# A hybrid sequence block: the modulation's matrix as TensorE's stationary float32 operand

## The chip, the cores and the metric

The kernel runs on one core of one Trainium2 chip. The metric is the device time of one execution in microseconds (us), the median of the runs shown.

## The reference

The block takes 2048 latent tokens `x` and 256 context tokens `ctx`, each of 1024 channels. A condition vector gives shift, scale and gate by one matrix product, once for `c` and once for `c_ctx`; the normed tokens are scaled and shifted by them, projected, mixed by four branches (a gated linear recurrence, a short convolution, a Fourier transform, a state space model) and projected back; the gate scales what is added to `x`.

```python
def adaln(cvec, ada_w, ada_b):
    m = jax.nn.silu(cvec) @ ada_w + ada_b
    m = m.reshape(-1, 1, 3 * D_MODEL)
    return jnp.split(m, 3, axis=-1)
...
shift, scale, gate = adaln(c, ada_w[l], ada_b[l])
h = rmsnorm(x, norm_w[l]) * (1.0 + scale) + shift
out, _, _ = mix(h, lp, rows, rg_st, ssd_st)
x = x + gate * out
```

`ada_w` is 1024 x 3072 in float32: 8 MB for shift and scale, 4 MB for the gate.

## The kernel before, in words

All large products run on TensorE (PE) as three products of float32r operands, `mm3` (L141 to L144): each float32 operand is split into a high part (a copy by ScalarE, `copy_hi`, L139) and a rest (a subtraction by VectorE or GpSimd), and high by high, high by rest and rest by high are summed in PSUM. Every instruction of the program is put in order on its engine when the kernel is compiled, by a scheduler that estimates times (`schedule_with_timeline_sim=True`); each engine then runs its own queue strictly in that order. Loads and stores are all issued from SyncE's queue (`ld`, L134).

**First stage.** The shift and scale columns come in eight blocks `k` of 1 MB (`ada_load`, two loads of 512 KB each), each with 128 shift and 128 scale columns for channels 128k to 128k+127. Two blocks share one of the 16 KB slots `H2` to `H5`. `ada_block` (L273) splits a block into slot `H6` or `H7`: in two halves of four row tiles, ScalarE copies the high part, VectorE subtracts three row tiles and GpSimd one (L281). The conditions stand still in PE: 4 columns (the high parts and the rests of `silu(c)` and `silu(c_ctx)`, `sil4`) for the matrix' high part (L283, 8 products of 256 moving columns) and 2 columns for its rest (L285, 8 more). The sum, 4 rows of 256, is copied to SBUF (L287) and transposed in two pieces (L289) into the bank `apt`, where three small VectorE operations (L292 to L294) turn it into `mod[k]`: shift, and norm weight times (1 + scale).

`to_h` (L298) then transposes channels 128k to 128k+127 of 512 normed tokens (four PE transposes, L301), applies `mod[k]` (`hr`, L305 or L307) and splits the result (`h_hi`, L139; `h_lo`, L309). In the loop over `k`, `ada_block(k)`, `to_h(k)` and nine products of three weight blocks with these 512 tokens (`mm3` into three accumulating banks) follow each other in the program. Behind the loop come the context's tokens (`xc`, loaded into slot `H2`), the next 512 tokens (`x1`, loaded into slot `H4`, which the blocks 4 and 5 held), and further products. Their loads stand behind the last block's in SyncE's queue.

**The gate's stage.** The gate's 1024 columns are worked out much later, beside the state space model's chain of states (L750 on): for each half of the columns and each of eight row tiles, 256 KB of the matrix are loaded (`gst`, two buffers), split by ScalarE and GpSimd (L214) and multiplied by `mm3` with a single stationary column (48 products of 512 moving columns). The sum lies in a bank of tag `bb`, of which there are two; before it, the same tag serves the products of L715 and L730. The row is added to the bias (L759) and stored.

Of the kernel before, what the change touches and what calls it, by code (L numbers as in the profile page):

```python
# [8 lines left out]
F32 = mybir.dt.float32  # L9
# [6 lines left out]
T = 2048  # L16
# [17 lines left out]
def constants():  # L34
# [5 lines left out]
    # channel transform: [cos 0..64 | sin 0..63], with the ortho norm and the gate's half  # L40
# [6 lines left out]
    # token transform: rows in blocks (window of 256, parity)  # L47
# [10 lines left out]
    # [par*4+w][cos/sin][128][f] -> split f into two tiles  # L58
# [11 lines left out]
def layout(x, c, ctx, c_ctx, ada_w, ada_b, norm_w, w_in, w_out, rg_conv_w, rg_conv_b, rg_gate_a_w, rg_gate_a_b,  # L70
# [7 lines left out]
    # [block of columns k][row within 128][rows / 128][shift | scale]  # L78
    a["ada"] = ca(ada_w[0][:, :2048].reshape(8, 128, 2, 8, 128).transpose(3, 1, 0, 2, 4).reshape(8, 128, 8, 256))
    a["adag"] = ca(ada_w[0][:, 2048:].reshape(8, 128, 1024))  # L80
    a["adabg"] = ca(ada_b[0][None, 2048:])
# [40 lines left out]
def build(tc, A, out):  # L122
# [23 lines left out]
    def softplus(pl, x, n, dst, scale_in=1.0, tag=None, bufs=None):  # L146
        """dst = log(1 + exp(scale_in * x)) for a [128, n] tile, exact also where it is small."""
# [27 lines left out]
    def mbank(four):  # L175
        """a bank for a projection; with four, of those of the transposes too"""
        nbank[0] += 1
        return bank("tr" if four and nbank[0] % 2 else "mm")
# [7 lines left out]
    # ---------------------------------------------------------------- constants  # L186
# [20 lines left out]
    # ---------------------------------------------------------------- weight blocks  # L207
# [3 lines left out]
    def split(hi, lo, raw, eng):  # L211
        """raw (float32) as a high part and a rest, both of 12 bits"""
        copy_hi(hi, raw)
        eng.tensor_tensor(lo, raw, f32(hi), SUB)  # L214
# [20 lines left out]
    # ---------------------------------------------------------------- adaLN shift and scale  # L235
# [10 lines left out]
    def norm_rows(xt):  # L246
        """scales the rows of xt [128, 1024] by 1/rms"""
        junk = q1.tile([128, 1024], BF16, name="junk")
        ss, rs = one("ss"), one("rs")
        act.activation(junk, xt, AF.Square, accum_out=ss)  # L250
        dve.tensor_scalar(rs, ss, 1.0 / D, EPS, MUL, ADD)
        pool.tensor_tensor(rs, rs, mhalf, ALU.pow)
        dve.tensor_scalar(xt, xt, rs, None, MUL)
        return xt

    # high and low part of the four columns side by side: one pass over the matrix' high part serves both
    sil4 = cst.tile([128, 8, 4], F32R, name="sil4")
    copy_hi(sil4[:, :, 0:2], sil)
    dve.tensor_tensor(sil4[:, :, 2:4], sil, f32(sil4[:, :, 0:2]), SUB)
# [4 lines left out]
    # [k][:, who] = shift, norm_w * (1 + scale)  # L264
# [7 lines left out]

    def ada_block(ar, k):  # L273
        hl = H16(f"ada{k}", 6 + k % 2, F32R, (2, 8, 256))
        pa = bank("ba")
        for i in range(2):
            s4 = slice(4 * i, 4 * i + 4)
            copy_hi(hl[:, 0, s4], ar[:, s4])
            for j, eng in ((0, dve), (1, pool)):
                r = slice(4 * i + 3 * j, 4 * i + 3 + j)  # L280
                eng.tensor_tensor(hl[:, 1, r], ar[:, r], f32(hl[:, 0, r]), SUB)  # L281
            for j in range(4 * i, 4 * i + 4):
                pe.matmul(pa[0:4, :256], sil4[:, j], hl[:, 0, j], start=(j == 0), stop=False)  # L283
            for j in range(4 * i, 4 * i + 4):
                pe.matmul(pa[0:2, :256], sil4[:, j, 0:2], hl[:, 1, j], start=False, stop=(j == 7))  # L285
        arow = q1.tile([4, 256], F32, name="arow", tag="arow", bufs=2)
        dve.tensor_copy(arow, pa[0:4, :256])  # L287
        for j in range(2):
            pe.transpose(apt[:, 8 * k + 4 * j:8 * k + 4 * j + 4], arow[:, 128 * j:128 * (j + 1)], ident[0:4, 0:4])  # L289
        av = apt[:, 8 * k:8 * k + 8].rearrange("p (j w) -> p w j", w=4)  # L290
        m = mod[k]
        dve.tensor_tensor(m, av[:, 0:2], adab[:, k, None, :].to_broadcast([128, 2, 2]), ADD)  # L292
        dve.tensor_tensor(m, m, av[:, 2:4], ADD)
        dve.tensor_scalar(m[:, :, 1], m[:, :, 1], cols[:, C_NW + k:C_NW + k + 1], None, MUL)  # L294

    # ---------------------------------------------------------------- normed, modulated, transposed tokens
# [30 lines left out]
    def conv_silu(pl, b, projs, n, emit, nb=3):  # L327
        """causal-ish convolution of 4 taps and silu over consecutive tiles of n tokens, each then given to emit"""
# [48 lines left out]
    # ---------------------------------------------------------------- first columns: RG-LRU input, context  # L377
# [30 lines left out]
    # the first tile of tokens and three blocks of weights run along with the columns of the modulation's matrix  # L408
# [9 lines left out]
    x1 = H16("x1", 4, F32, (4, 1024))  # L418
# [25 lines left out]
    # dt of the context, by columns  # L444
# [45 lines left out]
    # ---------------------------------------------------------------- RG-LRU  # L490
# [13 lines left out]
    def rg_front(us, n, e2):  # L504
        """Units of n tokens, at most one of either direction, each (blk, d, gate weights, source, conv, keep, init):
        the decays, the gated inputs and, in e2, the squares of these inputs' factors. A unit with conv starts from
        raw columns; their convolution goes to keep."""
        u = r2("r_u", 2)
        al = slice(us[0][1], us[-1][1] + 1)
        for blk, d, g, src, conv, keep, init in us:  # L510
            if conv:
                # two columns before and one after, zero beyond the ends
# [37 lines left out]
    def rg_back(us, n, e2, a, v, spans):  # L550
        """half the states of the units; the second to pass over a span of tokens adds the first one's"""
# [45 lines left out]
    for first in units:  # L597
        # two at a time, for the sake of one square root
# [14 lines left out]
    # ---------------------------------------------------------------- z and dt  # L613
    with pool_of("qz", left) as qz:
        for half in range(2):
            wzs = []
            # the first three in the slots of a weight block that is not in use
# [26 lines left out]
    # ---------------------------------------------------------------- SSD input columns  # L644
# [5 lines left out]
    # ---------------------------------------------------------------- SSD: steps, decays, entering states from the right  # L650
# [23 lines left out]
    def states(xs, xw):  # L674
        """state that a chunk adds, in PSUM [128 (g n), 256 (h p)]"""
# [12 lines left out]
    with pool_of("sp", right) as sp:  # L688
# [36 lines left out]
        # cumulative sums as rows [(chunk, head), token]  # L725
# [21 lines left out]
        # the output gate's modulation  # L747
        for n in range(2):
            s = slice(512 * n, 512 * (n + 1))
            p = bank("bb")  # L750
            for k in range(8):
                g3 = [sp.tile([128, 512], t, name=f"gst{i}", tag=f"gst{i}", bufs=2 if i == 0 else 1)
                      for i, t in enumerate((F32, F32R, F32R))]
                ld(g3[0], A["adag"][k][:, s])
                split(g3[1], g3[2], g3[0], pool)
                mm3(p[0:1], sil4[:, k, 0:1], sil4[:, k, 2:3], g3[1], g3[2], k == 0, k == 7)
            gr = sp.tile([1, 512], F32, name="gr", tag="gr")
            ld(gr, A["adabg"][:, s])
            dve.tensor_tensor(gr, gr, p[0:1], ADD)  # L759
            st(gate_d[:, s], gr)  # L760
# [8 lines left out]
    # ---------------------------------------------------------------- Fourier mixing  # L769
# [7 lines left out]
    for kind in range(2):  # L777
# [16 lines left out]
        for par in range(2):  # L794
            for w in range(4):
                # tokens t = 256 w + par + 2 m and their mirror images T - t
# [56 lines left out]
    for ft_ in range(2):  # L853
# [34 lines left out]
        n1 = NF if ft_ == 0 else 255      # f0 .. 512  # L888
        n2 = NF if ft_ == 0 else 254      # f0 .. 511 for the mirrored half
        lo1 = 1 if ft_ == 0 else 0        # no mirror image of f = 0  # L890

        for un in range(2):
# [7 lines left out]
            for (mn, pl_, n, at, back) in ((ap_, ae, n1, f0, T - f0), (am, ao, n2, 1024 + f0, 1024 - f0)):  # L900
# [6 lines left out]
                if at == f0:  # L907
                    # Y_P[f] = U, Y_Q[f] = V, Y_P[T-f] = V, Y_Q[T-f] = U
# [4 lines left out]
                else:  # L913
                    # Y_P[1024-f] = U, Y_P[1024+f] = V, Y_Q swapped
# [3 lines left out]
        # the Q of channel 0 is channel 64, on its own  # L918
# [14 lines left out]
    # ---------------------------------------------------------------- SSD, by chunks  # L933
# [31 lines left out]
    def ssd_head(c):  # L965
        """scores, decays and entering states of 128 tokens"""
# [5 lines left out]
        # the groups' C twice, on either half of the partitions  # L972
# [5 lines left out]
        # scores of the groups, transposed, masked for either direction  # L978
# [8 lines left out]
        # next state  # L987
# [4 lines left out]
        # entering states  # L992
        y = d2("y", bufs=2)
        pool.tensor_tensor(h64(y), h64(xs[:, 0:512]), bc(dskip, 64), MUL)
        for g in range(2):
            r = slice(64 * g, 64 * g + 64)
            s = slice(256 * g, 256 * g + 256)
            # high part of the entering states on their own partitions, the rest on the other half
# [13 lines left out]
        for g in range(2):  # L1012
            cs2 = []
            for d in range(2):
# [3 lines left out]
                # min(ci - cs, 0), and for the other direction its negative  # L1018
# [18 lines left out]
    def ssd_tail(c):  # L1037
        """the branch's normed output of 128 tokens, transposed"""
# [6 lines left out]
        # gate, norm  # L1045
# [31 lines left out]
    # ---------------------------------------------------------------- short gated convolution  # L1077
# [3 lines left out]
    def gate(p, pl):  # L1081
        """(1 + tanh(p/2)) * p: twice silu"""
# [55 lines left out]
    # ---------------------------------------------------------------- last gate, output weights  # L1138
# [3 lines left out]
    def ysplit(b, q, yr, yhl):  # L1142
        """the columns 4q .. 4q+4 (of 128) of the gated outputs of 128 tokens"""
# [4 lines left out]
    def oproj(yhl, q, ps_, cs, first, last):  # L1148
        """their part of the output projection, columns by columns"""
# [129 lines left out]
```

## Time and profile before

| what | value |
|---|---|
| median of 3 runs | 1653.36 us (1651.04 to 1655.83) |
| profiled execution, first to last instruction | 1656.3 us |
| PE busy | 1569.4 us (95%), 7906 matmuls |
| VectorE, ScalarE, GpSimd busy | 1053.3, 714.9, 564.3 us |
| DMA | 220.93 MB, mean 133 GB/s |

The page gives no time for the profiled execution besides its span. A matmul's busy time runs from its start to the modelled end of its result; the next one starts before that, so back to back the distance of two starts is what a matmul costs. PEld is the loading of a stationary operand, which runs beside the matmul before it. The granted clock (PEclk) is TensorE's: 1.00 is 2.4 GHz and 0.50 is 1.2 GHz.

### The profile page before, as it was taken

What the parts mean: (1) busy time and instruction counts of PE and PEld (TensorE: products, weight loads), DVE (VectorE), ACT (ScalarE), POOL (GpSimd) and SP (SyncE); (2) the same over time, 40 slices, a digit from 0 to 9 for tenths busy, and PEclk for the clock granted to TensorE, in tenths of its full rate; (3) what the DMA queues carried; (4) which work ended last, traced back from release to release, by engine and by line L of the source; (5) the groups of instructions that cost most, each with busy time, mean ns of one, the idle gap of its engine ahead of it and who ended that gap; (6) DMA issues with size and microseconds to landing.
All of it is one profiled execution on the core that took longest, in us unless ns stands there. A gap on an engine that the chain in (4) does not pass through costs nothing. (4 is left out here: it accounts for less than half of the span.)

```text
span 1656.3 us, 22749 instructions
## 1 busy us (share of the span) xinstructions
PE 1569.4 (95%) x7906; PEld 1271.5 (77%) x7906; DVE 1053.3 (64%) x1837; ACT 714.9 (43%) x1383; POOL 564.3 (34%) x536
## 2 busy tenths in 40 slices
PE   6899999899899999899999999898988999999998
PEld 3687899777788778666788888785766777777787
DVE  7765354698986657644168653437468777878653
ACT  5654046557465536211222324424345544545432
POOL 5533123312211422343315345334423424243310
PEclk9999999999999999999999999999999999999999
DMA  8424232323332231454222236657575655555532
GB/s 328 153 87 135 87 99 92 106 90 104 124 116 71 83 121 58 148 156 128 77 79 61 87 109 179 174 161 233 165 254 171 183 146 171 146 170 148 162 105 70
DMA packets 182257, 220.93 MB, mean 133 GB/s; under 512 B 20183, under 2 KB 118905, under 8 KB 182142
## 3 DMA queue, kind: packets, MB, share of 16 engines
q1 hardware_dynamic: 182142, 219.48, 42.8%
q8 instruction: 62, 1.02, 0.3%
q14 instruction: 53, 0.43, 0.1%
HBM read 155.40 MB, written 64.03 MB: 132 GB/s over the span
## 5 line engine op out<-in xcount | busy, mean ns | idle before, releaser
L142 PE MATMUL ps_mm<-h_hi,whi 128*128 128x512 f32 x696 | 276.9, 401 | 5.6 <-ACT craw L347 4.5
L143 PE MATMUL ps_mm<-h_lo,whi 128*128 128x512 f32 x696 | 278.7, 400 | 1.8 <-DVE h_lo L309 1.0
L144 PE MATMUL ps_mm<-h_hi,wlo 128*128 128x512 f32 x696 | 278.3, 400 | 0.0
L142 PEld LDWEIGHTS ps_mm<-h_hi,whi 128*128 128x128 f32 x696 | 133.1, 192 | 36.2 <-ACT craw L347 5.4
L143 PEld LDWEIGHTS ps_mm<-h_lo,whi 128*128 128x128 f32 x696 | 133.3, 192 | 31.6 <-DVE h_lo L309 2.2
L144 PEld LDWEIGHTS ps_mm<-h_hi,wlo 128*128 128x128 f32 x696 | 133.6, 192 | 28.9 <-issue 1.4
L142 PE MATMUL ps_tr<-h_hi,whi 128*128 128x512 f32 x384 | 151.6, 395 | 0.0
L143 PE MATMUL ps_tr<-h_lo,whi 128*128 128x512 f32 x384 | 151.5, 395 | 0.0
L144 PE MATMUL ps_tr<-h_hi,wlo 128*128 128x512 f32 x384 | 151.1, 394 | 0.0
L1153 PE MATMUL ps_mm<-wo_hi,oyhl 128*128 128x512 f32 (+1 forms) x272 | 106.9, 393 | 7.5 <-ACT oyhl L139 7.5
L139 ACT ACTIVATE whi<-wraw 128x512 fp32r<-128x512 f32 (+1 forms) x77 | 49.6, 645 | 143.4 <-DMA wraw<-wblk 98.4
L1155 PE MATMUL ps_mm<-wo_hi,oyhl 128*128 128x512 f32 (+1 forms) x272 | 106.2, 391 | 2.8 <-DVE oyhl L214 2.7
L1154 PE MATMUL ps_mm<-wo_lo,oyhl 128*128 128x512 f32 (+1 forms) x272 | 106.9, 393 | 0.0
L1009 POOL TENSOR_TENSOR y<-y,e 128x256 f32<-128x256 f32 x32 | 35.6, 1114 | 195.3 <-DVE e L1008 195.3
L1154 PE MATMUL ps_tr<-wo_lo,oyhl 128*128 128x512 f32 (+1 forms) x256 | 100.4, 392 | 0.0
L1155 PE MATMUL ps_tr<-wo_hi,oyhl 128*128 128x512 f32 (+1 forms) x256 | 100.0, 390 | 0.0
L1153 PE MATMUL ps_tr<-wo_hi,oyhl 128*128 128x512 f32 (+1 forms) x256 | 99.1, 387 | 0.0
L214 POOL TENSOR_TENSOR wlo<-wraw,whi 128x512 fp32r<-128x512 f32 (+1 forms) x40 | 61.7, 1543 | 97.3 <-ACT whi L139 81.8
L142 PEld LDWEIGHTS ps_tr<-h_hi,whi 128*128 128x128 f32 x384 | 72.8, 190 | 16.8 <-issue 2.1
L143 PEld LDWEIGHTS ps_tr<-h_lo,whi 128*128 128x128 f32 x384 | 72.6, 189 | 16.4 <-issue 1.7
L144 PEld LDWEIGHTS ps_tr<-h_hi,wlo 128*128 128x128 f32 x384 | 72.6, 189 | 15.6 <-issue 1.1
L139 ACT ACTIVATE oyhl<-oyr 128x512 fp32r<-128x512 f32 x68 | 42.6, 627 | 96.2 <-PE ps_tr L1155 72.6
(365 smaller groups left out, 3847.9 us busy)
## 6 DMA issues: line engine op xcount, KB each, us to landing
wraw<-wblk SPq DMA_DIRECT2D x74, 256.0 KB, 3.0
oyr<-ycat SPq DMA_DIRECT2D x68, 256.0 KB, 3.4
ci<-cst_d SPq DMA_DIRECT2D x64, 256.0 KB, 3.5
xs<-xsb_d SPq DMA_DIRECT2D x31, 320.0 KB, 3.0
adar<-ada SPq DMA_DIRECT2D x16, 512.0 KB, 10.2
hf_d<-r_v SPq DMA_DIRECT2D x32, 256.0 KB, 2.2
ycat<-gy SPq DMA_DIRECT2D x32, 256.0 KB, 2.4
wo_raw<-wout SPq DMA_DIRECT2D x16, 512.0 KB
```

What stands on the lines that cost most here:

```text
L139: act.activation(dst, src, AF.Copy)
L142: pe.matmul(ps, wh, xh, start=start, stop=False)
L143: pe.matmul(ps, wh, xl, start=False, stop=False)
L144: pe.matmul(ps, wl, xh, start=False, stop=stop)
L214: eng.tensor_tensor(lo, raw, f32(hi), SUB)
L1009: pool.tensor_tensor(y[:, s], y[:, s], e[:, 0:256], ADD)
L1153: pe.matmul(p, yhl[:, 0, j], wo_hi[q][:, j, c0:c1], start=first and j == 0, stop=False)
L1154: pe.matmul(p, yhl[:, 0, j], wo_lo[q][:, j, c0:c1], start=False, stop=False)
L1155: pe.matmul(p, yhl[:, 1, j], wo_hi[q][:, j, c0:c1], start=False, stop=last and j == 3)
```

## The change

The matrix becomes the stationary operand, in float32 and unsplit, and the conditions' two columns move (`columns`): for each block and each of shift and scale, eight products of a 128x128 piece with 2 moving columns, which land with channels on the partitions, as `mod[k]` wants them. The splits, the copy of the 4 rows, the transposes and one of the small additions are gone. The gate is done in the same way with one moving column: the matrix is laid out in eight blocks of 128 columns, loaded by 512 KB each into two buffers, and the resulting 128x8 columns are transposed once and stored. The slots `H6` and `H7` are now free during the first stage, and `x1` is loaded into `H6` instead of `H4`. The other lines of the diff take comments out.

```diff
-    a["adag"] = ca(ada_w[0][:, 2048:].reshape(8, 128, 1024))
-    a["adabg"] = ca(ada_b[0][None, 2048:])
+    a["adag"] = ca(ada_w[0][:, 2048:].reshape(8, 128, 8, 128).transpose(2, 1, 0, 3))
+    a["adabg"] = ca(ada_b[0][2048:].reshape(8, 128).T)
...
-    sil4 = cst.tile([128, 8, 4], F32R, name="sil4")
-    copy_hi(sil4[:, :, 0:2], sil)
-    dve.tensor_tensor(sil4[:, :, 2:4], sil, f32(sil4[:, :, 0:2]), SUB)
...
+    def columns(p, w, n):
+        for j in range(8):
+            pe.matmul(p, w[:, j], sil[:, j, 0:n], start=(j == 0), stop=(j == 7))
+
     def ada_block(ar, k):
-        hl = H16(f"ada{k}", 6 + k % 2, F32R, (2, 8, 256))
-        pa = bank("ba")
         for i in range(2):
-            s4 = slice(4 * i, 4 * i + 4)
-            copy_hi(hl[:, 0, s4], ar[:, s4])
-            for j, eng in ((0, dve), (1, pool)):
-                r = slice(4 * i + 3 * j, 4 * i + 3 + j)
-                eng.tensor_tensor(hl[:, 1, r], ar[:, r], f32(hl[:, 0, r]), SUB)
-            for j in range(4 * i, 4 * i + 4):
-                pe.matmul(pa[0:4, :256], sil4[:, j], hl[:, 0, j], start=(j == 0), stop=False)
-            for j in range(4 * i, 4 * i + 4):
-                pe.matmul(pa[0:2, :256], sil4[:, j, 0:2], hl[:, 1, j], start=False, stop=(j == 7))
-        arow = q1.tile([4, 256], F32, name="arow", tag="arow", bufs=2)
-        dve.tensor_copy(arow, pa[0:4, :256])
-        for j in range(2):
-            pe.transpose(apt[:, 8 * k + 4 * j:8 * k + 4 * j + 4], arow[:, 128 * j:128 * (j + 1)], ident[0:4, 0:4])
-        av = apt[:, 8 * k:8 * k + 8].rearrange("p (j w) -> p w j", w=4)
+            columns(apt[:, 4 * k + 2 * i:4 * k + 2 * i + 2], ar[:, :, 128 * i:128 * i + 128], 2)
+        av = apt[:, 4 * k:4 * k + 4].rearrange("p (i w) -> p w i", w=2)
         m = mod[k]
-        dve.tensor_tensor(m, av[:, 0:2], adab[:, k, None, :].to_broadcast([128, 2, 2]), ADD)
-        dve.tensor_tensor(m, m, av[:, 2:4], ADD)
+        dve.tensor_tensor(m, av, adab[:, k, None, :].to_broadcast([128, 2, 2]), ADD)
...
-    x1 = H16("x1", 4, F32, (4, 1024))
+    x1 = H16("x1", 6, F32, (4, 1024))
...
-        for n in range(2):
-            s = slice(512 * n, 512 * (n + 1))
-            p = bank("bb")
-            for k in range(8):
-                g3 = [sp.tile([128, 512], t, name=f"gst{i}", tag=f"gst{i}", bufs=2 if i == 0 else 1)
-                      for i, t in enumerate((F32, F32R, F32R))]
-                ld(g3[0], A["adag"][k][:, s])
-                split(g3[1], g3[2], g3[0], pool)
-                mm3(p[0:1], sil4[:, k, 0:1], sil4[:, k, 2:3], g3[1], g3[2], k == 0, k == 7)
-            gr = sp.tile([1, 512], F32, name="gr", tag="gr")
-            ld(gr, A["adabg"][:, s])
-            dve.tensor_tensor(gr, gr, p[0:1], ADD)
-            st(gate_d[:, s], gr)
+        gp = bank("bb")
+        for k in range(8):
+            gst = sp.tile([128, 8, 128], F32, name="gst", tag="gst", bufs=2)
+            ld(gst, A["adag"][k])
+            columns(gp[:, k:k + 1], gst, 1)
+        gr = sp.tile([128, 8], F32, name="gr", tag="gr")
+        ld(gr, A["adabg"])
+        dve.tensor_tensor(gr, gr, gp[:, 0:8], ADD)
+        gp = bank("bb")[0:8, 0:128]
+        pe.transpose(gp, gr, ident)
+        gt = sp.tile([8, 128], F32, name="gt", tag="gt")
+        dve.tensor_copy(gt, gp)
+        st(gate_d.rearrange("o (k n) -> (o k) n", n=128), gt)
```

## Rows read from the trace of the kernel before

**Rows 1.** The page: busy time of each engine (share of the span) and instructions.

```profile
PE 1569.4 (95%) x7906; PEld 1271.5 (77%) x7906; DVE 1053.3 (64%) x1837; ACT 714.9 (43%) x1383; POOL 564.3 (34%) x536
```

**Rows 2.** Windows: length, busy us (instructions) of PE, PEld, DVE, ACT, POOL; clock, DMA share, GB/s.

```profile
23.30:30.10 6.80, 3.97 (x24) 2.03 (x22) 6.39 (x8) 1.65 (x2) 6.07 (x4) 1.00 1.03 418
...
33.50:64.90 31.40, 29.06 (x174) 20.79 (x172) 27.50 (x50) 23.98 (x39) 22.83 (x21) 1.00 0.53 188
64.90:100.00 35.10, 31.54 (x226) 27.72 (x225) 22.14 (x37) 17.38 (x34) 14.59 (x16) 1.00 0.26 83
```

**Rows 3.** Groups by line and form, 0 to 100 us: busy us, mean ns | idle before.

```profile
L281 DVE TENSOR_TENSOR ada<-adar,ada 128x768 fp32r<-128x768 f32 x16 | 21.2, 1333 | 1.8 <-ACT ada L139 1.5 <-issue 0.3
L281 POOL TENSOR_TENSOR ada<-adar,ada 128x256 fp32r<-128x256 f32 x16 | 19.1, 1210 | 8.4 <-ACT ada L139 8.4
L139 ACT ACTIVATE ada<-adar 128x1024 fp32r<-128x1024 f32 x16 | 16.2, 1049 | 6.5 <-PE ps_ba L285 3.8 <-DMA adar<-ada 2.7
```

**Rows 4.** Timeline of the first stage: start, us, merged instructions; L283's ns, min/median/max.

```profile
15.51 1.06 ACT L139 ACTIVATE ada<-adar 128x1024 fp32r<-128x1024 f32 x1 [0.16 <-DMA adar<-ada]
...
20.61 1.05 PE L283 MATMUL ps_ba<-ada,sil 128*4 128x256 f32 x4
...
24.04 0.63 PE L283 MATMUL ps_ba<-ada,sil 128*4 128x256 f32 x4
...
64.30 0.40 PE L143 MATMUL ps_bb<-h_lo,whi 128*128 128x512 f32 x1
64.53 0.39 PE L144 MATMUL ps_bb<-h_hi,wlo 128*128 128x512 f32 x1
64.77 0.60 PE L301 MATMUL ps_tr<-ident,xc 128*128 128x128 f32 x4
...
L283 PE MATMUL ps_ba<-ada,sil x64: 276/279/562, 7.6 to 51.6; 128*4 128x256 f32 x64
```

**Rows 5.** Line 786 (float32, 64 products in the program): ns, min/median/max; its timeline.

```profile
L786 PE MATMUL ps_ba<-ft,wft x128: 217/275/275, 839.4 to 934.4; 128*128 128x65 f32 x64, 128*128 128x64 f32 x64
...
839.36 1.89 PE L786 MATMUL ps_ba<-ft,wft 128*128 128x65 f32 x16
841.06 0.48 PE L143 MATMUL ps_tr<-h_lo,whi 128*128 128x512 f32 x1
```

**Rows 6.** Timeline at 1125 us, clock 0.50, dense products.

```profile
1125.15 0.63 PE L142 MATMUL ps_mm<-h_hi,whi 128*128 128x512 f32 x1
...
1125.58 0.63 PE L143 MATMUL ps_mm<-h_lo,whi 128*128 128x512 f32 x1
```

**Rows 7.** Windows as rows 2: two stretches, what followed each; one matmul of either.

```profile
1067.80:1071.20 3.40, 1.93 (x12) 1.07 (x10) 1.03 (x2) 1.66 (x4) 1.85 (x3) 1.00 0.81 262
1071.20:1074.60 3.40, 2.91 (x8) 2.45 (x9) 0.69 (x1) 1.31 (x5) 1.17 (x2) 0.50 0.75 206
327.10:330.50 3.40, 1.62 (x8) 1.00 (x6) 3.40 (x6) 1.45 (x2) 0.10 (x1) 1.00 0.41 154
330.50:333.90 3.40, 2.40 (x12) 1.93 (x13) 3.40 (x6) 2.77 (x5) 1.00 (x1) 1.00 0.22 80
...
1069.40 0.28 PE L144 MATMUL ps_ba<-ct,zz 128*128 128x258 f32 x1
...
328.33 0.39 PE L144 MATMUL ps_mm<-h_hi,wlo 128*128 128x512 f32 x1
```

**Rows 8.** The queue of SyncE: what it waited for, 0 to 200 us (us, times, longest).

```profile
SPq L134 <- DVE ada L281: 11.9, 1, 11.9
```

**Rows 9.** The gate's stage: its window (as rows 2) and its timeline.

```profile
712.80:835.00 122.20, 122.20 (x533) 84.04 (x533) 44.05 (x73) 22.89 (x37) 48.97 (x40) 1.00 0.41 121
...
682.06 0.91 SPq L134 DMA_DIRECT2D gst<-adag  x2
...
715.50 0.47 PE L142 MATMUL ps_bb<-gst,sil 128*1 128x512 f32 x1
```

**Rows 10.** The tile of the gate's matrix: ns, min/median/max.

```profile
L214 POOL TENSOR_TENSOR gst<-gst,gst x16: 1272/1296/1718, 687.3 to 824.1; 128x512 fp32r<-128x512 f32 x16
```

## The prediction

> **What bounds the kernel now.** I read the page's busy times first: PE is busy for 95% of the span, the next engine, VectorE, for 64% [rows 1]. So an edit counts by what it does to PE's queue, or to a stretch in which PE waits. I then read windows of the two stages that the change touches. In the first stage (to 64.9 us, the end of the first tile's last product [rows 4]) PE does not bound alone. DMA still moves 418 GB/s up to 30 us; from 33.5 to 64.9 us PE, VectorE, ScalarE and GpSimd are all busy for 23 to 29 of 31.4 us, each waiting for another in turn [rows 2]. In the gate's stage PE is busy without a gap, 122.2 of 122.2 us [rows 9], so there nothing but PE's own work counts.
>
> **The price of one product.** Line 786 is the change's form: float32, 128x128 standing still, few columns (64 or 65) moving. The program has 64 such products (8 pieces x 4 groups x 2 kinds); the trace has 128 matmuls [rows 5], each with its load, so "unsplit" holds for the program only: the chip runs each product as two pairs of load and matmul. Sixteen of them start at 839.36 us and the next matmul at 841.06 us, so 1.70 / 16 = 0.106 us for a pair, 0.21 us for a product. I take this for 2 moving columns and for 1 as well: the load of 128 columns sets it, and that is the same. By the Trainium skill (FP8 and Floating Point Precision, TensorE Precision Notes) true float32 takes 4 passes through PE; were each a load of its own, the first stage would come out 27 us worse than below. The trace shows two loads for a product, so I leave it there.
>
> **The price by clock.** At the lower of the two levels of the granted clock everything on PE takes about twice as long: products of 512 columns start every 0.43 us at 0.50 [rows 6], against a start every 0.23 us at 64.3 us [rows 4]. Four of L283 took 1.05 us at 20.6 us and 0.63 us at 24.0 us [rows 4], so PE also starts the kernel at the lower level. The trace has no load-bound stretch at the lower level; my estimate for a pair there is 2 x 0.106 = 0.213 us.
>
> **First stage, removed.** ScalarE loses 16.2 us, VectorE 21.2 us and two small operations a block, GpSimd 19.1 us [rows 3]. PE loses 128 matmuls of 256 columns: four take 0.63 us together and one alone 0.28 us [rows 4], so a start every (0.63 - 0.28) / 3 = 0.117 us and 14.9 us at the upper level; and 16 transposes of 4 columns, which I leave unpriced. The loads of `x1` no longer wait for blocks 4 and 5, an 11.9 us wait of SyncE's queue [rows 8].
>
> **First stage, added.** 8 blocks x 2 x 8 products x 2 pairs = 256 pairs: 32 pairs a block, 3.4 us at the upper level, 6.8 us at the lower. In all 27 or 54 us, where 15 went. Whether that lies on the path is a sum over PE's queue, since the other engines now have little left. Block 0 lands first and takes 6.8 us at most; I let it be over by 15.5 us, when block 1 is complete [rows 4]. From there PE has 7 blocks, 8 sets of four transposes (four in 0.60 us [rows 4], so (0.60 - 0.28) / 3 = 0.11 us each: 0.44 us, or 0.88 at the lower level) and 8 sets of nine products (9 x 0.23 = 2.07 or 9 x 0.43 = 3.87 us). DMA is past its full rate after 33.5 us [rows 2], so the data are there long before PE is through, and PE sets the end:
> - at the upper level throughout: 15.5 + 7 x 3.4 + 8 x 2.51 = 59.4 us;
> - at the lower throughout: 15.5 + 7 x 6.8 + 8 x 4.75 = 101.1 us;
> - before: 64.9 us.
>
> **Which level?** The trace shows no stretch of loads with next to no columns moving. What it shows is which stretches came before a fall. From 1067.8 to 1071.2 us PE was busy for 1.93 us, and the clock then stood at 0.50; from 327.1 to 330.5 us PE was busy for less, 1.62 us, loaded as much (1.00 against 1.07 us), and the clock stayed at 1.00. The first held 12 matmuls of 258 columns, the second 8 of 512 [rows 7]: the one that fell was the busier one, with fewer columns through the array. A block of the modulation is 32 pairs of 2 columns, the emptiest of all by that measure. So I take it that the level falls in the blocks and is won back in the nine dense products between them, and set the end halfway, at 80.3 us: 15.4 us later than before.
>
> What follows, from 64.9 to 100 us before, has PE busy for 31.54 of 35.10 us [rows 2]. The context's tokens and `x1` are now loaded, normed and waiting long before PE comes to them (their cover is PE's own backlog), so the idle 3.6 us go. First stage: +15.4 - 3.6 = **+11.8 us**; ends: 59.4 - 64.9 - 3.6 = -9.1 us and 101.1 - 64.9 - 3.6 = +32.6 us.
>
> **Gate, removed and added.** 48 products of 512 columns at 0.23 us (11.0 us) go; 8 blocks x 8 products x 2 pairs = 128 pairs at 0.106 us (13.6 us) and one transpose (0.1 us) come: +2.7 us on an engine without a gap. GpSimd's 16 x 1.30 = 20.7 us [rows 10] and ScalarE's copies give nothing, PE covers them; were PE not the bound, GpSimd's share in the chain of states would count, up to those 20.7 us. The two first blocks are loaded from 682 us on, but their bank, of the tag that L730 uses too, served the first product only at 715.5 us [rows 9]; so they run in one go, 32 pairs or 3.4 us, and I put half of that on top for a fall: 1.7 us. Later blocks come singly, among dense products. The bias' load and the store change their shape and have no one waiting. Gate: **+4.4 us**; ends +2.7 us and, all at the lower level, +16.3 us.
>
> **Sum.** 11.8 + 4.4 = +16.2 us on a span of 1656.3 us: 1672.5 us. The median of the runs is 0.18% below the profiled span, so 1669.5 us. A measurement of this kernel can tell about 0.3% (5 us) from no change.
>
> **Rivals.**
> - **The level holds.** Loads back to back keep the upper level after the start; PE is never idle with this backlog. Then the stage ends 9.1 us earlier; without the backlog I give back the 3.6 us of idle: -5.5 + 2.7 = -2.8 us, 1650.5 us, and without giving them back 1647 us. It decides the case if loads alone keep the clock up. For it: ahead of the falls at 30 and 1071 us PE idled for 6.80 - 3.97 = 2.8 and 3.40 - 1.93 = 1.5 us [rows 2, 7], and here it would not idle. Against it: the busier of the two stretches is the one that fell. Chance 0.22, of which 0.10 are faster, 0.10 no change and 0.02 slower. The Trainium skill (TensorE: Matmul & The Clock Gate, Part 1) says that the clock follows how busy PE has been and that idle gaps bring it down, which is this rival; the trace agrees for the idle 2.8 us and speaks against it in the pair of stretches [rows 7].
> - **The level never comes back** in the first stage: +32.6 + 4.4 us, 1690 us. For it: the scheduler may scatter the nine products among the blocks. Against: between 20.6 and 24.0 us the level rose out of products of 256 columns and transposes [rows 4], and nine products of 512 are denser. Chance 0.06, slower.
> - **Another order decides.** The scheduler sees other costs and may place the later work differently everywhere; or the relief of VectorE shortens later stages too. No row prices it; a few us either way, around the sums above. Chance 0.07: 0.04 faster, 0.02 no change, 0.01 slower.
> - **The forecast**: the level falls and returns, three tenths to three quarters of the way from the one end to the other, 1661 to 1680 us. Chance 0.65, slower.
>
> Summed: faster 0.14, no change 0.12, slower 0.74. The range that leaves out 2 in 10 runs from 1648 us (the level holds) to 1684 us (the lower level for five sixths of the way).
>
> **What would show it.** Right: 256 loads and 256 matmuls of the new line, pairs 0.106 us apart at a clock of 1.00 and 0.21 us at 0.50; windows between 15 and 80 us with clocks between the two; no idle of PE from 15 us on; the last product of the first tile at about 80 us; VectorE and GpSimd idle beside it; 128 pairs for the gate, with a fall at about 718 us. Wrong: a clock of 1.00 through blocks that follow each other, a pair far from 0.106 us, or PE waiting in the first stage for `mod` or for DMA.

## The result, and the profile after

The changed kernel takes 1671.09 us, the median of 4 runs, against 1652.20 us for the kernel before, measured again beside it. The ratio is 1.0108 (95% interval 1.008 to 1.0135), or 17.8 us (13 to 22 us) more. Forecast were 1669.5 us and 16.2 us more. The two profiled executions are only 9.8 us apart (spans 1666.1 and 1656.3 us): that of before lies about 0.2% above its median, that of after is the fastest of its four. So the traces below say where the time went, and the ratios how much it is.

PE's row of the page after, beside [rows 1]: 29.8 us more busy, 193 more matmuls, and 20.0 us less idle (86.9 us before, 66.9 us after).

```profile
PE 1599.2 (96%) x8099; PEld 1319.2 (79%) x8099; DVE 1027.1 (62%) x1804; ACT 689.9 (41%) x1350; POOL 527.6 (32%) x504
```

**First stage.** The new line's groups, and the timeline of PE, merged by line (start, us, instructions):

```profile
L273 PEld LDWEIGHTS ps_bb<-sil,adar 128*128 128x128 f32 x256 | 45.0, 266 | 8.4 <-DVE sp L160 6.9
L273 PE MATMUL ps_bb<-sil,adar 128*128 128x2 f32 x256 | 42.8, 297 | 6.9 <-DMA adar<-ada 6.9
```

```profile
17.64 5.12 PE L273 MATMUL ps_bb<-sil,adar 128*128 128x2 f32 x24
22.62 1.09 PE L288 MATMUL ps_tr<-ident,xt 128*128 128x128 f32 x4
...
46.13 2.21 PE L273 MATMUL ps_bb<-sil,adar 128*128 128x2 f32 x16
48.20 0.64 PE L288 MATMUL ps_tr<-ident,xt 128*128 128x128 f32 x4
48.67 5.38 PE L273 MATMUL ps_bb<-sil,adar 128*128 128x2 f32 x32
53.91 1.09 PE L288 MATMUL ps_tr<-ident,xt 128*128 128x128 f32 x4
...
64.01 3.81 PE L273 MATMUL ps_bb<-sil,adar 128*128 128x2 f32 x32
67.67 0.88 PE L288 MATMUL ps_tr<-ident,xt 128*128 128x128 f32 x3
...
75.34 2.06 PE L273 MATMUL ps_bb<-sil,adar 128*128 128x2 f32 x18
77.27 0.41 PE L288 MATMUL ps_tr<-ident,xc 128*128 128x128 f32 x2
...
80.76 0.48 PE L288 MATMUL ps_tr<-ident,xc 128*128 128x128 f32 x2 [1.98 <-DVE hr L292]
81.42 1.22 PE L143 MATMUL ps_mm<-h_hi,whi 128*128 128x512 f32 x2 [0.18 <-ACT h_hi L140]
...
84.98 0.39 PE L145 MATMUL ps_bb<-h_hi,wlo 128*128 128x512 f32 x1
```

As in [rows 5], 128 products make 256 pairs. At 17.64 us 24 of them take 4.98 us, 0.208 us for a pair: the lower level. At 64.01 us 32 take 3.66 us, 0.114 us for a pair: the upper level. Windows of the same stage, columns as in [rows 2]:

```profile
15.50:43.50 28.00, 28.00 (x113) 25.94 (x112) 6.87 (x8) 7.33 (x11) 9.80 (x7) 1.00 1.02 392
43.50:50.30 6.80, 6.80 (x43) 6.15 (x41) 1.94 (x6) 4.41 (x9) 1.28 (x2) 1.00 0.13 40
50.30:57.10 6.80, 6.80 (x29) 6.32 (x29) 5.50 (x13) 4.40 (x9) 5.89 (x7) 0.50 0.15 48
57.10:67.40 10.30, 10.30 (x81) 9.73 (x80) 3.74 (x7) 2.21 (x4) 1.79 (x2) 1.00 0.13 47
67.40:70.80 3.40, 3.40 (x13) 2.81 (x13) 1.08 (x3) 1.41 (x2) 0.00 (x0) 0.50 0.47 153
70.80:77.30 6.50, 6.50 (x47) 5.91 (x45) 1.95 (x6) 4.33 (x7) 1.65 (x3) 1.00 0.63 246
77.40:85.40 8.00, 5.18 (x20) 3.64 (x19) 5.17 (x12) 3.60 (x9) 3.23 (x4) 0.79 0.00 0
85.40:97.90 12.50, 12.21 (x105) 11.37 (x103) 4.09 (x9) 2.58 (x6) 1.50 (x3) 1.00 0.24 85
```

PE has no gap from 15.5 to 77.4 us, the end of the last block's pairs. The clock column prints 1.00 from 15.5 to 43.5 us, where the pairs are 0.20 to 0.21 us apart: ahead of the level's first recorded rise that column can't be relied on, the distance of the starts can. The level rises within the 16 pairs from 46.13 us on (2.07 us: 1.8 would be all upper, 3.3 all lower), is at 0.50 from 50.3 us, up again, at 0.50 from 67.4 us, up again, and at 0.50 once more from 81.0 to 84.4 us (hence 0.79 in the window from 77.4 us on). VectorE and GpSimd, busy for 88% and 73% of such a stretch before [rows 2], now have little to do.

The first tile does not end with the last block's pairs: its last nine products run from 81.42 us on, and the last of them ends at 85.4 us (64.9 us before). Between the two PE idles for 2.8 us, and what it waits for is `mod[7]`. The columns of the last block are there at 77.4 us, but VectorE turns them into `mod[7]` only at 79.44 us: norms of tokens that are needed later stand ahead of it in VectorE's queue, the second of them only after a wait of 0.73 us for GpSimd. The scaled rows (`hr`), their high part and the products follow one behind the other:

```profile
77.23 0.75 DVE L254 TENSOR_SCALAR xt<-xt,rs 128x1024 f32<-128x1024 f32 x1 [0.73 <-POOL rs L253]
78.77 0.75 DVE L254 TENSOR_SCALAR xt<-xt,rs 128x1024 f32<-128x1024 f32 x1 [0.73 <-POOL rs L253]
79.44 0.15 DVE L280 TENSOR_TENSOR mod<-ps_bb,adab 128x4 f32<-128x4 f32 x1
79.90 0.81 DVE L292 TENSOR_SCALAR hr<-ps_tr,mod 128x512 f32<-128x512 f32 x1
80.74 0.63 ACT L140 ACTIVATE h_hi<-hr 128x512 fp32r<-128x512 f32 x1 [2.01 <-DVE hr L292]
```

The rest of the context's part, up to the two 16-column transposes of its time steps, ends at 97.9 us (82.9 us before). It takes 12.5 us with 0.3 us idle; before, it took 18.0 us with 3.6 us idle:

```profile
64.90:82.90 18.00, 14.44 (x109) 12.15 (x107) 11.60 (x23) 7.98 (x17) 7.88 (x9) 1.00 0.32 103
```

So the first tile ends 20.5 us later, the part behind it is 5.5 us shorter, and the first stage is 15.0 us longer in this profile.

**Gate.** Timeline and windows of the changed kernel:

```profile
726.21 3.77 PE L273 MATMUL ps_bb<-sil,gst 128*128 128x1 f32 x32
729.91 1.97 PE L665 MATMUL ps_ba<-xw,xs 128*64 128x256 f32 x8
```

```profile
726.10:729.60 3.50, 3.50 (x34) 3.50 (x33) 0.29 (x1) 0.46 (x1) 2.08 (x2) 0.99 0.57 162
729.60:733.00 3.40, 3.40 (x14) 2.06 (x14) 1.70 (x4) 0.00 (x0) 0.00 (x0) 0.50 0.80 283
733.00:736.50 3.50, 3.50 (x17) 2.89 (x16) 0.00 (x0) 0.00 (x0) 0.88 (x1) 1.00 0.71 220
```

The blocks come two at a time, 32 pairs in 3.7 us, and the level falls right behind them. This happens four times, from 729.6, 739.8, 753.5 and 763.7 us on.

The order of the work differs between the two kernels as well, most of all behind the gate's start. So whatever is compared below is compared by the ratio of the runs, or between the same two pieces of work.

### The profile page after: what moved, and what is told of

It is laid out like the page before. It is cut to its first block, busy times and chain, and to the rows that moved or that the text cites. A ratio compares the mean times of both kernels' runs of the same rounds, so it can differ in the third digit from the quotient of the medians.

```text
span 1666.1 us, 22985 instructions
## 1 busy us (share of the span) xinstructions
PE 1599.2 (96%) x8099; PEld 1319.2 (79%) x8099; DVE 1027.1 (62%) x1804; ACT 689.9 (41%) x1350; POOL 527.6 (32%) x504
## 4 chain that ended last, share of the span: by engine, by line
PE 67%; DVE 13%; DMA 9%; ACT 5%; issue 3%; SPq 1%; POOL 1%; POOLq 0%; DVEq 0%; ACTq 0%
PE ps_mm L143 7%; PE ps_mm L144 7%; PE ps_mm L145 6%; PE ps_tr L145 4%; PE ps_tr L143 4%; PE ps_tr L144 4%; PE ps_mm L1141 3%; PE ps_mm L1140 3%; PE ps_mm L1142 3%; PE ps_tr L1141 3%; PE ps_tr L1142 3%; PE ps_tr L1140 3%; PE ps_bb L273 3%; DVE r_v L543 2%; PE ps_bb L1031 2%
## 5 line engine op out<-in xcount | busy, mean ns | idle before, releaser
L1140 PE MATMUL ps_mm<-wo_hi,oyhl 128*128 128x512 f32 (+1 forms) x272 | 107.9, 397 | 4.7 <-ACT oyhl L140 4.7
L145 PEld LDWEIGHTS ps_tr<-h_hi,wlo 128*128 128x128 f32 x384 | 73.3, 191 | 16.2 <-issue 1.5
```

The costliest lines, as they stand in the source:

```text
L145: pe.matmul(ps, wl, xh, start=False, stop=stop)
L1140: pe.matmul(p, yhl[:, 0, j], wo_hi[q][:, j, c0:c1], start=first and j == 0, stop=False)
```

## The experiments

Twelve runs were made, each beside the kernel before on the same chip. The theory is that of the forecast: PE's own work sets the time, and the pairs with hardly any moving columns bring its clock down. The rivals are that the order of the later work decides, and that the level has nothing to do with the columns.

| run | edit | us | before | ratio (95%) |
|---|---|---|---|---|
| e1 | first stage alone, 2 columns | 1669.37 | 1649.07 | 1.0126 (1.010 to 1.0152) |
| e9 | first stage alone, 128 columns | 1650.40 | 1647.84 | 1.0014 (1.0001 to 1.0026) |
| e2 | gate alone, 1 column | 1647.60 | 1649.07 | 0.9991 (0.998 to 1.0001) |
| e6 | gate alone, 128 columns | 1640.96 | 1648.92 | 0.9951 (0.9935 to 0.9967) |
| e5 | gate alone, one buffer | 1640.10 | 1648.92 | 0.9950 (0.9934 to 0.9965) |
| e10 | gate alone, one buffer, 128 columns | 1637.82 | 1647.84 | 0.9939 (0.9921 to 0.9956) |
| e3 | changed, 32 columns in both | 1660.78 | 1649.07 | 1.0076 (1.0056 to 1.0096) |
| e8 | changed, 64 columns in both | 1653.48 | 1648.92 | 1.0026 (1.0012 to 1.004) |
| e4 | changed, 128 columns in both | 1646.54 | 1649.07 | 0.9983 (0.9972 to 0.9995) |
| e11 | changed, once more | 1673.14 | 1647.84 | 1.0143 (1.0116 to 1.0171) |
| e7, e12 | changed, x1 in H4 | 1673.64, 1672.02 | 1648.92, 1647.84 | 1.0159 (1.0139 to 1.0179), 1.0149 (1.0127 to 1.0172) |

### One part alone

e1 keeps the old gate with its splits, e2 the old first stage; no other line differs.

```diff
 # e1: after, with
+    sil4 = cst.tile([128, 8, 4], F32R, name="sil4")
...
-            columns(gp[:, k:k + 1], gst, 1)
+                mm3(p[0:1], sil4[:, k, 0:1], sil4[:, k, 2:3], g3[1], g3[2], k == 0, k == 7)
 # e2: before, with
-                mm3(p[0:1], sil4[:, k, 0:1], sil4[:, k, 2:3], g3[1], g3[2], k == 0, k == 7)
+            columns(gp[:, k:k + 1], gst, 1)
```

Expected of e1:

> Only the first stage is changed (matrix standing still, x1 in H6); the gate is split and multiplied as before. Theory A, PE's own work and its clock: the first stage ends as in the changed kernel, its first tile's last product at about 77 us instead of 64.9, with one to three stretches of clock 0.50 between 45 and 90 us, and the context's small transposes at about 98 us instead of 83; nothing is lost at the gate, so the sum is 12 to 15 us over the kernel before, about 1665 us. Rival B, the other order of the later work decides: the first stage is as late, but the total lands anywhere from 5 us under to 19 us over the kernel before, with the difference arising behind 100 us.

Expected of e2:

> Only the gate is changed; the first stage is that of the kernel before (last product of the first tile at about 65 us). Theory A: 128 pairs in place of 48 products cost 2.7 us, and each run of 32 pairs (two blocks, as the two buffers come in twos) brings a stretch of clock 0.50 of 3.4 us or more, 1.7 us or more each; four of them make 6.8 us. Sum +9.5 us, about 1662 us. Rival B: the gate costs what its pairs cost, +2.7 us or less since GpSimd and ScalarE lose their splits, so 1650 to 1655 us, and the falls in the changed kernel come from something else.

Measured: e1 is 20.8 us slower than before (0.0126 x 1649.07), more than expected, and its profile has the context's transposes at 104.6 us, 21.7 us late; by 715 us the lag is still 17.6 us. So the loss arises in the first stage, not in the order behind it. e2 is not slower (-1.5 us, -3.3 to +0.2). My 9.5 us for the gate was a miss, although the four falls are there; two windows of e2, right behind its first two blocks, and the stage from the last product with the second mask to the first product of the output projection:

```profile
711.10:715.20 4.10, 4.10 (x39) 4.01 (x39) 0.29 (x1) 0.49 (x1) 2.08 (x2) 1.00 0.62 201
715.20:718.60 3.40, 3.40 (x13) 2.09 (x10) 1.70 (x4) 0.00 (x0) 0.00 (x0) 0.50 0.86 291
...
711.10:1198.10 487.00, 474.81 (x2496) 392.85 (x2495) 254.26 (x417) 142.82 (x322) 180.06 (x151) 0.98 0.45 137
```

That stage took 487.0 us before as well. The two ratios multiplied, 1.0117, give that of the whole change.

### More moving columns

The conditions are repeated along a dimension of stride zero, so that 32, 64 or 128 columns move behind each load; the first two (or one) are used. Loads, matmuls and the output stay.

```diff
-            pe.matmul(p, w[:, j], sil[:, j, 0:n], start=(j == 0), stop=(j == 7))
+            pe.matmul(p, w[:, j], sil[:, j, None, 0:n].to_broadcast([128, r, n]), start=(j == 0), stop=(j == 7))
...
-            columns(apt[:, 4 * k + 2 * i:4 * k + 2 * i + 2], ar[:, :, 128 * i:128 * i + 128], 2)
+            columns(pa[:, 128 * i:128 * i + 128], ar[:, :, 128 * i:128 * i + 128], 2, 64)
```

That is the form with 128 (`pa` is a bank of tag `ba`); with 32 the sums still fit into `apt`, and the order of the work is nearly that of the changed kernel. With 64 and 128 the order differs.

> The changed kernel, but with 32 moving columns for 2 (the two conditions repeated) in the first stage and 32 for 1 in the gate; as many loads and matmuls, in nearly the same order. Theory A (the clock falls because next to no columns move): a pair stays at 0.106 us, since its load sets it, and the falls become fewer or, if 32 columns are still too few, stay; 1658 to 1671 us. Rival C (the clock falls because of the loads, or for a reason that has nothing to do with the columns): the same falls at the same places and 1671 us.

> The changed kernel, but with 128 moving columns in the first stage and in the gate. Theory A: no clock of 0.50 in the modulation once the level has risen, neither in the first stage nor behind the gate's blocks; a pair takes 0.106 us if its load still sets it, or up to 0.12 us; the first tile's last product at 60 to 66 us, the gate at +2.7 us: 1647 to 1656 us. Rival C: the falls stay and the total is 1665 to 1675 us. Rival B: the first stage gets faster, but the total stays within 5 us of the changed kernel, because the order decides.

> As the run with 128 moving columns, but with 64 in the first stage and in the gate. Theory A, what counts is how much of a pair's time columns move: between the run with 32 columns (falls as with 2) and that with 128 (none): if 64 are enough, 1645 to 1650 us and a rise before 25 us; if not, falls remain and the first tile ends at 65 to 75 us, 1652 to 1660 us. Rival C: the time does not follow the columns, and comes out above the run with 32 or below the run with 128.

Measured: a window of e3, then e8's window from its first rise to the context's first transpose, then two of e4, around a run of 32 pairs and behind it:

```profile
50.80:57.60 6.80, 6.80 (x28) 6.11 (x28) 4.30 (x11) 6.74 (x13) 4.15 (x5) 0.50 0.12 42
```

```profile
25.70:61.20 35.50, 35.50 (x262) 32.90 (x262) 11.65 (x29) 15.72 (x27) 13.98 (x13) 1.00 0.57 214
```

```profile
53.80:57.40 3.60, 3.60 (x35) 3.60 (x34) 2.37 (x7) 3.60 (x7) 1.21 (x3) 1.00 0.22 77
57.40:60.80 3.40, 3.10 (x19) 2.40 (x16) 3.24 (x5) 2.62 (x6) 1.73 (x2) 1.00 0.62 229
```

With 32 columns the first stage falls where it fell with 2, and its context part ends at 98.0 us, as with 2 (97.9). At the gate it has 10.2 us at 0.50 instead of 17.0 us; where the rest of its 5 us (by the ratios) comes from, its one profile does not show. With 64 and 128 there is no fall in the first stage's modulations nor at the gate (e4 has one later, at 73.5 us, after 3.4 us in which PE was busy for 1.8 us), though the runs of 32 pairs are still there and PE's loads are as busy (3.60 of 3.60 us in e4). The pair's price hardly moves: 32 pairs from start to next start are 3.66 us with 2 columns and 3.58 us with 128. So rival C in its plain form, that the loads bring the level down whatever moves, has fallen. The bank and the order of the work change with 64 and 128 columns as well, and are not tried apart from them. That e8 is some 7 us slower than e4 (by the ratios) is not explained by either place, since both are without falls there; it stays open.

### The first stage with the level held

e9 is e1 with 128 columns: the same edit as above, in the first stage only.

> Only the first stage is changed, with 128 moving columns for 2; the gate is split and multiplied as before. It stands beside the run with only the first stage changed and 2 columns (1669 us, first stage 21.7 us late). Theory A, the clock of the first stage is what that run lost: no clock of 0.50 in the first stage behind its rise, the first tile's products done at about 58 us, the context's small transposes at 83 to 85 us, total 1647 to 1653 us. Rival B, the order of the later work decides: the first stage is in time, but the total stays over 1658 us.

Measured: 1.0014 against 1.0126. Of the 20.8 us, 18.5 (0.0112 x 1649) hang on the number of moving columns (with the bank and the order that come with it). Windows and timeline of e9:

```profile
18.60:58.30 39.70, 38.91 (x291) 36.26 (x291) 11.96 (x29) 15.78 (x26) 14.73 (x12) 1.00 0.66 259
58.30:83.50 25.20, 20.22 (x132) 15.81 (x131) 15.92 (x29) 12.59 (x26) 8.78 (x12) 1.00 0.41 147
```

```profile
54.33 3.74 PE L274 MATMUL ps_ba<-sil,adar 128*128 128x128 f32 x32
...
64.99 0.44 PE L290 MATMUL ps_tr<-ident,xc 128*128 128x128 f32 x2 [1.44 <-DVE rs L252]
...
66.43 0.39 PE L145 MATMUL ps_bb<-h_hi,wlo 128*128 128x512 f32 x1
...
73.65 0.44 PE L290 MATMUL ps_tr<-ident,xc 128*128 128x128 f32 x2 [1.29 <-DVE hr L294]
```

After 18.6 us there is no fall in the first stage (one, at 15.1 us, came ahead, after 3.4 us in which PE was busy for 1.7 us). The last block's pairs are over at 58.1 us, where I had expected the first tile's products to be done; but 18 of these still follow, mixed with the context's transposes and with waits for norms and scaled rows, and the last ends at 66.8 us, 1.9 us later than before. PE idles for 5.0 us from 58.3 us on, and the stage ends at 83.5 us (82.9 before): in time, but not ahead.

### The gate's falls

e5 takes one of the two buffers away, so that 16 pairs come at a time; e6 widens the columns to 128 (in two banks of four blocks); e10 does both. All keep the first stage of before.

```diff
-            gst = sp.tile([128, 8, 128], F32, name="gst", tag="gst", bufs=2)
+            gst = sp.tile([128, 8, 128], F32, name="gst", tag="gst", bufs=1)
```

> The kernel of the run with only the gate changed, but with one buffer for the gate's matrix instead of two, so that its blocks come one at a time (16 pairs, 1.8 us) with 17 to 33 other entries of PE's queue between them instead of two at a time (32 pairs, 3.6 us). Theory A, the level falls behind a long enough run of pairs: no clock of 0.50 behind the eight single blocks, or at most one or two of them, where there were four stretches of 3.4 us; PE saves up to 4 x 1.7 = 6.8 us less what the single buffer makes it wait, so 1641 to 1648 us. Rival: a fall behind each block, eight stretches, 1654 us; or the falls go and the time stays at 1648 us, because the chain of states, not PE, sets the end of that stage.

> The kernel of the run with only the gate changed, but with 128 moving columns for 1; the blocks still come two at a time. Theory A: the four stretches of clock 0.50 at the gate go, the pairs stay at 0.11 us, and the stage from the last product with the second mask to the first product of the output projection, 487.0 us with one column, takes 480 to 484 us; total 1641 to 1646 us. Rival: the falls go but the time stays at 1647.6 us.

> Only the gate is changed, with one buffer and 128 moving columns, both edits that took the falls away. Theory A: there is hardly a fall left that they could save twice, so no more than the one stretch at 735 us of the run with one buffer (1.7 us): 1637 to 1641 us. Rival: the two edits gain independently of the clock, and their gains of 7 us each add up to 1633 us.

Measured: the same stage as in e2 above, for e6, then e5 (with its one stretch at 0.50), then e10:

```profile
710.60:835.00 124.40, 124.40 (x726) 102.18 (x725) 71.50 (x121) 23.86 (x51) 42.95 (x34) 1.00 0.43 135
...
710.60:1190.80 480.20, 468.88 (x2495) 389.60 (x2494) 257.57 (x418) 143.30 (x322) 180.33 (x151) 0.99 0.45 139
```

```profile
734.60:738.00 3.40, 3.40 (x11) 1.42 (x8) 2.24 (x5) 0.72 (x1) 1.18 (x1) 0.50 0.94 275
...
714.20:1188.20 474.00, 469.29 (x2496) 391.36 (x2495) 249.87 (x417) 143.95 (x322) 179.87 (x151) 0.99 0.46 142
```

```profile
712.30:1184.50 472.20, 466.94 (x2495) 389.22 (x2494) 248.51 (x418) 144.16 (x322) 179.46 (x151) 0.99 0.46 143
```

Either edit makes the kernel some 7 us faster than e2, and both together no more than 2 us on top (by the ratios). They take the same falls away: PE is busy for 474.8 us of e2's stage and for 468.9 and 469.3 us here. In e5 PE's idle time in the stage shrinks as well (12.2 to 4.7 us), which is order, not clock; that stage is 13 us shorter than e2's and the kernel only 7 us, so part of it is given back outside, and how much of e5's gain is the falls' is not shown. e10 is the fastest version of all, 0.61% under the kernel before.

### The place of x1, and the changed kernel again

```diff
-    x1 = H16("x1", 6, F32, (4, 1024))
+    x1 = H16("x1", 4, F32, (4, 1024))
```

> The changed kernel with x1 back in slot H4, which the blocks 4 and 5 hold; otherwise nearly the same order. Forecast's view: PE has a backlog in the first stage, so x1's place is worth nothing: 1671 us within 4 us. Rival D: x1's load waits for the last products of blocks 4 and 5 at about 60 us and PE then waits for x1's rows behind the context: 3 to 10 us more, 1674 to 1681 us.

> The changed kernel with x1 in slot H4, once more, to stand beside the changed kernel on the same chip. Forecast's view: the same as the run beside it within 4 us. Rival D: x1's load waits for blocks 4 and 5 and PE for x1, 3 to 10 us more than the run beside it.

> The changed kernel itself, once more, beside the next run. Forecast's view: 1664 to 1676 us; falls at the same places of the order of the work in the first stage, though when the level first rises may differ (46.9 us in the changed kernel's profile, 60.8 us in the run with only the first stage changed, whose first stage has the same order), and with it the end of the stage, 15 to 22 us later than before.

Measured: e7 came out at 1.0159 where the changed kernel had 1.0108, which left rival D alive; so both ran once more side by side. There they are the same, 1.0149 and 1.0143. The slot is worth nothing that can be measured.

e11's profile is the slower of the changed kernel's two, with a span of 1677.9 us. PE does the same work in the same order as in the profile after, but the level first rises later; timeline and windows:

```profile
50.30 6.83 PE L273 MATMUL ps_bb<-sil,adar 128*128 128x2 f32 x32
56.99 1.09 PE L288 MATMUL ps_tr<-ident,xt 128*128 128x128 f32 x4
...
61.47 1.84 PE L273 MATMUL ps_bb<-sil,adar 128*128 128x2 f32 x16
...
94.63 0.63 PE L145 MATMUL ps_bb<-h_hi,wlo 128*128 128x512 f32 x1
```

```profile
64.60:81.60 17.00, 17.00 (x69) 15.48 (x67) 2.29 (x6) 3.16 (x5) 1.26 (x1) 0.50 0.19 68
81.60:88.50 6.90, 6.24 (x46) 5.53 (x44) 3.22 (x8) 4.34 (x9) 2.20 (x4) 0.99 0.37 140
```

The run of 32 pairs that took 5.24 us up to the next start in the profile after, at 48.67 us, takes 6.69 us here at 50.30 us, all at the lower level. At the 16 pairs of 61.47 us (57.96 us in the profile after) e11, now at the upper level too, is 3.5 us behind; then it stays at 0.50 for 17.0 us from 64.6 us on, where the profile after has 3.4 us from 67.4 us on, and the lag grows to 9.9 us. The first tile's last product ends at 95.3 us and the context's part at 107.9 us.

## Why the prediction was right, and where it was not

**The time, the direction and the mechanism** were right: PE's own work sets the time, and the level falls behind the pairs and comes back. The parts were not as well sized as the sum. The first stage cost 20.8 us (by e1's ratio) where 11.8 us were forecast, the gate -1.5 us (by e2's) where +4.4 us were; that the two misses cancel is luck.

**The price of a pair.** Forecast 0.106 us; measured 0.111 to 0.114 us (e2: 32 pairs from 711.25 to 714.81 us; after: 64.01 to 67.67 us), and 0.208 us at the lower level where I had estimated 0.213. The trace has two pairs a product, 256 for 128 products, as that of before had it. The Trainium skill (FP8 and Floating Point Precision, TensorE Precision Notes) speaks of four passes for true float32; how they are shared out between two pairs no run here shows.

**The end of the first tile.** The forecast put its last product halfway between 59.4 and 101.1 us, at 80.3 us. It ends at 85.4 us in the profile after, 92.1 us in e1 and 95.3 us in e11, that is 0.62, 0.78 and 0.86 of the way. The counts were right: 32 pairs are through by 15.5 us, 224 pairs and 72 products follow. Three things were not. The step "PE sets the end", since the other engines "now have little left", leaves out the wait for `mod[7]`: 2.8 us idle in the profile after, 2.4 us in e1, 1.9 us in e11. "PE waiting in the first stage for `mod`" was among the prediction's own signs of being wrong, and "no idle of PE from 15 us on" among those of being right. VectorE has little left by its busy time, but its queue is in order, and other work stood ahead of the one operation that PE needed. Then, part of the context's transposes (1.8 us in the profile after) runs ahead of the first tile's last products. And "halfway" was a choice that no row gave; in e1 and e11 PE spends more of the stage at the lower level. How much differs from one execution to the next. e9 comes near the case of the upper level throughout: 66.8 us with one early fall, where the sum has 59.4 us. Of these 7.4 us, 3.2 are idle time and 1.5 transposes of the context; the pairs are 1.5 us and the products 1.7 us dearer than in the sum, the tile's own transposes 0.6 us cheaper (each from its start to the next start).

**The falls.** Those at 50.3 and 67.4 us came out of the blocks and the level rose in the products behind them, as forecast. The first rise, within the pairs from 46.13 us on, and the fall at 81.0 us, during the wait for `mod[7]`, did not come that way.

**The idle 3.6 us** behind the first tile went as forecast: 0.3 us are left, and the part is 5.5 us shorter. It is in part a shift: PE now idles ahead of the tile's last products, and by their end it has started 10 of the context's 16 transposes (4 before). Together the first stage costs 15.0 us in the profile after (20.5 - 5.5, where the forecast has 15.4 - 3.6), 21.7 us in e1's and 25.0 us in e11's.

**The step that failed at the gate** is "later blocks come singly, among dense products". They come in twos, as the two buffers let them, and all four pairs of blocks bring a fall. That term was sized at 1.7 us; taking the falls away gains 6.6 us by e6, and 6.8 us by e5, which saves idle time as well (ratios against e2's). The other term, +2.7 us for the pairs, stands as work on PE (14.2 us against 11.5 us), but something gives back more: without falls (e6) the new gate is 8 us faster than the old one. Of that, the first 68 products of the chain of states (L678) are one part: PE is busy with them for 13.6 us before, where they stand among the gate's products (0.200 us each), and for 10.2 us in e6 (0.150 us each), where they run in groups of eight. PE's idle time in the stage is another, 13.7 us before and 11.3 us in e6. How much of the rest is GpSimd's relief, to which I had given nothing, and how much only another order, was not tried and stays open.

**The rivals.** "The level holds" is what e4 builds, by moving more columns: forecast 2.8 us faster, measured 2.8 us (0.9983). But its parts are off as the forecast's are, nothing gained by 83.5 us and a gain at the gate, so that the number agrees is luck. In the changed kernel the level did not hold, although PE was busy for 6.80 of 6.80 us ahead of the fall at 50.3 us, and without a gap for the 17 us at 0.50 in e11; ahead of the fall at 81.0 us it did idle, for 2.6 us. The Trainium skill (TensorE: Matmul & The Clock Gate, Part 1) says that the clock follows how busy PE has been and that idle gaps bring it down: the fall at 81.0 us agrees with it, the other two stretches do not, and there the measurement decides. "Another order decides" may explain e5's idle time and e8, but not the loss: e1's lag is there at the end of the first stage. "The level never comes back" did not happen.

## What to carry to other kernels

Price an operand swap on TensorE by loads as well as by columns, and then look at what it leaves the array to do between the loads: here an old line of the same form gave the pair's price within 8%, and in the first stage the number of moving columns, by the clock, decided 18 of the 21 us. Where a load sets the price of a pair, more moving columns (a repeated operand) cost next to nothing, and here they brought those 18 us back; shorter runs of such pairs, by one buffer instead of two, took the falls away at the gate. And an engine that has become idle can still keep the bottleneck waiting: look at what stands ahead in its queue of the one operation that the bottleneck needs, here two norms of later tokens ahead of `mod[7]`.

## What the runs showed of the hardware that was not expected

- PE stayed at the lower level although it never paused: pairs 0.20 to 0.21 us apart and products 0.43 us apart, without a gap, from 15.5 to 43.5 us after, and 6.69 us for 32 pairs as late as 50.30 us in e11. With this order of work the first rise came some 14 us apart (at about 47 us in one execution, at 61 us in the other); once both had the upper level, the second was 3.5 us behind, and with the longer fall that followed there the first tile's end moved by 10 us. The Trainium skill (TensorE: Matmul & The Clock Gate, Part 1) says that how many matmuls run before the first rise differs from run to run; the traces agree.
- A pair of float32 load and matmul takes 0.11 us whether 1, 2 or 128 columns move behind it (32 pairs in 3.56, 3.66 and 3.58 us).
- Taking a buffer away made a kernel faster: 0.9950 of the kernel before with one buffer for the gate's matrix (e5), 0.9991 with two (e2).
